# Conditioning products for the second layer's first norm: from the first layer's attention to behind its output projection

## The chip, the cores and the metric

The kernel runs on one core of one Trainium2 chip. The metric is the device time of one execution in microseconds (us); less is better. The core has a matrix engine (TensorE, PE in the views, with its weight loads as PEld), a vector engine (DVE), a scalar engine (ACT), GpSimd (POOL) and a sync engine (SP), which here issues most of the loads from DRAM. Each engine works through its own instructions in order and waits on semaphores for the others.

## The reference

A trunk of two layers over 512 latent tokens and 256 context tokens of width 1024. What matters here is where the conditioning enters:

```python
m = split((silu(c) @ w_ada[l] + b_ada[l]), 6)         # six vectors of 1024 for the latent stream
h = layer_norm(x) * (1 + m[1]) + m[0]                 # first norm, feeds the input projection
y = concat(pool, windowed attention, latent attention, gating)(h @ w_in[l]) @ w_out[l]
x = layer_norm_affine(ALPHA * x + m[2] * y)
f = square(relu((layer_norm(x) * (1 + m[4]) + m[3]) @ w_ff1[l])) @ w_ff2[l]
x = layer_norm_affine(ALPHA * x + m[5] * f)
```

The context stream does the same in the first layer with its own vector `c_ctx`; in the second layer it only needs m[0] and m[1]. `c` is known from the start, so the products with `w_ada` depend on nothing but their weights.

## The kernel before

All products are in float32 or in pairs of float32r halves, so that every weight block is loaded raw by SP (512 KB in one DMA), split on ACT (high half) and DVE (low half), and used three times by TensorE. Raw blocks go through a ring of four slots (tag `raw`); SP issues the next load when a slot is free again.

**Conditioning.** `ada_steps(l, g, ...)` computes 2048 of the 6144 columns of layer l: g = 0 holds the first norm's shift and scale, g = 1 the attention gate and the second norm's shift, g = 2 the second norm's scale and the feed-forward gate. It goes in 16 steps; each loads one raw block of `w_ada` (512 KB, tile `wada`) into the same ring of four and does 8 products on TensorE straight from it (16 matmul instructions in the trace), with no split. The sum lies in one PSUM bank (tile `ada`, a pool with one buffer), and DVE adds the bias (tile `badab`) when a part of it is done, into `adaA` (L250); that frees the bank. `ada_cols` turns the rows into columns with TensorE transposes (`adaT`) and DVE copies; `gate_rows` writes a gate to DRAM (`grow`, issued by SP).

**Where it is done.** The generator `conditioning()` in `run` hands out the steps while the units of attention are written: `fill(x, n)` takes steps up to a number that grows with the unit x. In the first layer these are the 16 steps of g = 1, the first 8 of g = 2, and the 16 of the second layer's g = 0, 40 in all (24 in the second layer). The other 8 steps of g = 2 are written after the output projection (`out_proj`, tiles `wo`), behind the norms `norm1`.

**What follows.** `norm1` runs on DVE, ACT and POOL, tile by tile (tiles `x`, `xc`, `xn`). Then `ffn` starts with `ff1_first`: `modT` transposes the normalised tiles on TensorE (tile `hT`), ACT scales them (`hh`, `hfull`), DVE takes the low half (`hl`), and the first 512 columns of the feed-forward product follow (tile `ff`, weights `w1z` already split). Seven more chunks of 512 follow, with weights through the ring (`raww`).

**What sets the order.** A scheduler of the framework orders the instructions of each engine when the kernel is built, from the order in which the code writes them and a simulated timeline; the order on an engine is then fixed.

Of the kernel before, what the change touches and what calls it, by code (L numbers as in the profile page):

```python
# [14 lines left out]
PSUM = bass.MemoryType.PSUM  # L15
DRAM = bass.MemoryType.DRAM
# [11 lines left out]
# layer norm of ALPHA x + y as that of x + y / ALPHA, with the guard scaled alike  # L28
# [19 lines left out]
class Trunk:  # L48
# [64 lines left out]
    def load(self, **kw):  # L113
        """a load by the sync engine; while self.chain is set, behind the one before."""
        i = self.nc.sync.dma_start(**kw)
        if self.chain is not None:
            if self.chain:
                self.after(i, self.chain[-1])
            self.chain.append(i)
        return i  # L120

# [10 lines left out]
    def split(self, hi, lo, src, scale=None):  # L132
        """hi + lo = src * scale, each half exact in fp32r."""
        nc = self.nc
        if scale is None:
            i = nc.scalar.activation(out=hi, in_=src, func=AF.Copy)
            nc.vector.tensor_tensor(out=lo, in0=src, in1=hi.bitcast(F32), op=ALU.subtract)
            return i
        else:
            nc.scalar.activation(out=hi, in_=src, func=AF.Copy, scale=scale)  # L140
            nc.vector.scalar_tensor_tensor(
                out=lo, in0=src, scalar=scale, in1=hi.bitcast(F32), op0=ALU.mult, op1=ALU.subtract
            )

    def load_w(self, pieces, shape, name, gate=None):
        """weights from DRAM, split in two fp32r halves; pieces: (slice of the tile, source)."""
        nc = self.nc
        raw = self.pr.tile(shape, F32, name=self.nm("raw" + name), tag="raw")
        for sl, src in pieces:
            self.load(out=raw[sl], in_=src)  # L150
        hi = self.pw.tile(shape, F32R, name=self.nm("hi" + name), tag="W")
        lo = self.pw.tile(shape, F32R, name=self.nm("lo" + name), tag="W")
        i = nc.scalar.activation(out=hi, in_=raw, func=AF.Copy)  # L153
        if gate is not None:
            self.after(i, gate)
        nc.vector.tensor_tensor(out=lo, in0=raw, in1=hi.bitcast(F32), op=ALU.subtract)  # L156
        return hi, lo

    def rstd(self, out, var, scale=1.0, eps=EPS):
        """(var * scale + eps) ** -0.5"""  # L160
        nc = self.nc
        v = self.S1("rv")
        nc.vector.tensor_scalar(out=v, in0=var, scalar1=scale, scalar2=eps, op0=ALU.mult, op1=ALU.add)
        nc.gpsimd.tensor_tensor(out=out, in0=v, in1=self.mhalf, op=ALU.pow)

    def stats(self, src, chunks, eps=EPS):
        """mean and 1/std of rows; src(i) gives the i-th chunk of at most 512 columns."""
        nc = self.nc
        st = self.S1("bst", 6 * chunks)
        for i in range(chunks):  # L170
            nc.vector.bn_stats(out=st[:, 6 * i:6 * i + 6], in_=src(i))  # L171
        mv = self.S1("bmv", 2)
        nc.vector.bn_aggr(out=mv, in_=st)
        rs = self.S1("brs")
        self.rstd(rs, mv[:, 1:2], eps=eps)
        return mv[:, 0:1], rs
# [39 lines left out]
    def ada_steps(self, l, g, res, parts=((0, 1, 2, 3),)):  # L216
        """2048 columns of silu(c) @ w_ada + b_ada for both streams, in steps: row 32 j + 16 stream,
        column 128 q + x holds feature 512 q + 128 j + x. The rows go to res[0]."""
# [38 lines left out]
    def ada_cols(self, a, name, plus_one, parts=((0, 1, 2, 3),), mc=None):  # L257
        """columns [feature, block, stream] out of the rows of ada; plus_one: halves that are scales."""
        nc = self.nc
        if mc is None:  # L260
            mc = self.pc.tile([128, 16, 2], F32, name=self.nm(name), tag=name, bufs=2)
        for part in parts:
            pt = self.PA("adaT")
            for i, q in enumerate(part):
                self.tr(pt[:, 128 * i:128 * i + 128], a[:, q, :])
                nc.vector.tensor_scalar(
                    out=mc[:, 4 * q:4 * q + 4, :],
                    in0=pt[:, 128 * i:128 * i + 128].rearrange("p (b r) -> p b r", r=32)[:, :, 0:32:16],
                    scalar1=1.0 if q // 2 in plus_one else 0.0, scalar2=None, op0=ALU.add,
                )  # L270
        return mc

    def gate_rows(self, a, half, streams):
        """1024-wide rows of ada to DRAM, over ALPHA."""
# [30 lines left out]
    def sum_sq(self, x, nm, junk, name):  # L305
        """sum of (x + nm) ** 2 of rows on the scalar engine."""
# [20 lines left out]
    def affine_ln2(self, x, g, b, dst, act):  # L327
        """x = affine layer norm of x, and the plain layer norm of that in dst; act: the latter on the scalar
        engine."""
# [22 lines left out]
    def modT(self, xn, t0, t1, shift, scale, h, kts=range(KT), two=False):  # L352
        """xn(i, kt): token tile i, features kt; fills h[kt] = hi, lo [feature, token]."""
        nc = self.nc
        n = 128 * (t1 - t0)
        for kt in kts:
            pt = (self.PF if two and kt % 2 else self.PA)("hT")
            last = None
            for i in reversed(range(t0, t1)):
                # the last token tile first, so that the bank is not held while it is awaited  # L360
# [56 lines left out]
    def rope(self, x, p0, p1, tab, shuf):  # L417
        """x [p0:p1, 512] in place."""
# [7 lines left out]
    def proj_T(self, l, hL, hC, c0, nf, evict, ctx_too, name):  # L426
        """feature-major columns c0.. of h @ w_in, nf tiles of 128."""
# [26 lines left out]
    def wb_units(self, l, k0, k1, ku, cols, name):  # L454
        """token-major weights of h @ w_in, split: [kt][hi, lo]."""
# [13 lines left out]
    def proj_tok(self, l, groups, cols, ku, evict, name, Ws=(), early=None):  # L469
        """token-major columns of h @ w_in; groups: lists of (h tiles, index in h, output number), each  # L470
        preceded by what prepares it; cols: column ranges."""
        n = sum(b - a for a, b in cols)
        Ws = list(Ws)
        if early is not None:
            # by halves of the features, as the conditioning comes in
# [37 lines left out]
    def softmax(self, S, lo, hi, keep, z=False):  # L513
        """rows of S[:, lo:hi] in PSUM; the first `keep` probabilities come back."""
# [21 lines left out]
    def probs_T(self, p, nb):  # L536
        """transposes the nb key blocks of p."""
# [15 lines left out]
    def pv(self, O, pTs, vs, q0):  # L553
        """O[64 * head : , q0 : q0 + 128] += sum over key blocks of v^T p^T for two heads."""
# [9 lines left out]
    def mixers(self, l, P, hL, hC, preps, fill, early):  # L564
# [6 lines left out]
        # cq and the gating half of the spatial-gating unit, token-major  # L571
# [26 lines left out]
        # pooling  # L598
        pool_finish = self.pool(l, P, hL, hC, yL, yC, full)
        # k and q of the windowed attention  # L600
# [47 lines left out]
        # u  # L648
# [9 lines left out]
        # v, ckv, kr token-major  # L658
# [15 lines left out]
        # spatial gating  # L674
        self.sgu(l, P, U, VG, yL, yC, full)

        # latent attention: normalised low-rank parts, feature-major
# [118 lines left out]
        # the work, one head and one tile of queries at a time  # L796
# [39 lines left out]
        # latent-attention operands are made ahead, between the units of the part before  # L836
# [134 lines left out]
    def ff1_z(self, l):  # L971
        """the weights of the first chunk, split in slots that are free between the phases; three slots
        take the eight blocks of a column tile."""
# [17 lines left out]
    def wb_z(self, l):  # L991
        """the first feature tiles of the weights of the first projection, likewise."""
# [20 lines left out]
    def xn_new(self, ends):  # L1013
        """room for a normalised token tile: a slot, and a third of another."""
# [12 lines left out]
    def out_weights(self, l):  # L1027
        """the first half of w_out, while attention ends."""
# [15 lines left out]
    def out_part(self, yL):  # L1044
        """next products of the first two token tiles that do not wait for the last heads."""
# [7 lines left out]
    def out_proj(self, l, yL, yC, x, xc, gl, gc, gate_inst):  # L1053
        """x += gate (y @ w_out), token-major."""
# [29 lines left out]
    def ffn(self, l, hL, hC, x, xc, rows2, mod2, done):  # L1084
# [40 lines left out]
        def ff1_first():  # L1125
            """the first chunk while the hidden state is still being made: token halves apart, in their
            own banks, so that the first does not wait for the second."""
# [78 lines left out]
    def bcast_rows(self, src, name):  # L1206
        """a parameter row on all partitions, loaded behind the scalar engine's work so far."""
# [5 lines left out]
    def run(self):  # L1213
# [53 lines left out]
        for l in range(DEPTH):  # L1267
# [4 lines left out]
            # conditioning that only the rest of the layer needs, between the units of attention  # L1272
# [3 lines left out]
            def conditioning():  # L1276
# [9 lines left out]
                if not last:  # L1286
                    yield from self.ada_steps(l + 1, 0, r)
                    cond["mc0"] = self.ada_cols(r[0], "mc0", (1,))
# [4 lines left out]
            def fill(x, n):  # L1293
                want = (x + 1) * (24 if last else 40) // (n - 4) + 1
# [7 lines left out]
            gr1, mc0 = cond["gr1"], cond.get("mc0")  # L1302
            # residual stream again
# [29 lines left out]
            # the second gate, while the first norm is awaited  # L1333
            for _ in cond["ada2"]:
                pass
            gr2 = self.gate_rows(cond["a2"], 1, ns)
            norm2 = []
# [12 lines left out]
            def done(j):  # L1350
                """token tile j has left the feed-forward part."""
# [87 lines left out]
```

## Time and profile before

| | |
|---|---|
| runs, us | 1599.86, 1599.83, 1595.42; median 1599.83 |
| profiled execution | span 1596.2 us from the first to the last instruction; no time of its own is listed for it |
| TensorE | busy 1519.9 us (95%) |
| DVE, ACT, POOL | busy 933.6, 573.8, 207.9 us |
| DMA | 169.94 MB, 106 GB/s on average |
| granted TensorE clock | 0.986 of 2.4 GHz on average |

The span falls into stages: projections of the first layer to about 160 us, its attention from 160 to 330, its output projection from 329.4 to 383.95, its feed-forward part from 386 to about 915, and then the same for the second layer, without context queries. Times in the rows are microseconds from the span's start.

### The profile page before, as it was taken

The page shows a single profiled execution, that of the slowest core. Times are in us where ns is not written, and L with a number is a line of the kernel's source. Part 1 is how long each engine was busy: PE and PEld are TensorE (multiplying, and loading weights), DVE is VectorE, ACT ScalarE, POOL GpSimd, SP SyncE. Part 2 cuts the span into 40 slices and gives each one's busy share as a digit, 9 for nine tenths or more (in the row PEclk, how much of TensorE's full clock was granted, in tenths as well). Part 3 has the DMA queues.
Part 4 walks back from the last instruction along what each step waited for, and adds up shares of the span by engine and source line. Part 5 has one row for each costly group of instructions (what it writes and reads, how often), then busy time and mean ns, then how long its engine had stood idle before and what let it go on. Part 6 is the DMA issues. An engine that isn't in the chain of part 4 may idle for free.

```text
span 1596.2 us, 23567 instructions
## 1 busy us (share of the span) xinstructions
PE 1519.9 (95%) x9480; PEld 1257.1 (79%) x9480; DVE 933.6 (58%) x1630; ACT 573.8 (36%) x1003; POOL 207.9 (13%) x217
## 2 busy tenths in 40 slices
PE   5999989999999999999999989998988999999996
PEld 3789767777888888888888868876767888888885
DVE  3484776457445445454454788577546555655557
ACT  4533445423631211312212166346534523223230
POOL 1011223224000000000000151124113000000003
PEclk9999999999999999999999999999999999999999
DMA  9432635363232121221212224260554332332321
GB/s 307 144 117 79 195 115 167 112 237 95 73 97 62 53 79 53 80 62 55 70 53 80 69 90 119 74 205 10 164 188 122 119 105 94 93 93 92 106 80 53
DMA packets 148069, 169.94 MB, mean 106 GB/s; under 512 B 8776, under 2 KB 96248, under 8 KB 147960
## 3 DMA queue, kind: packets, MB, share of 16 engines
q1 hardware_dynamic: 138488, 150.98, 30.4%
q10 hardware_dynamic: 9472, 17.45, 3.2%
q8 instruction: 75, 1.23, 0.3%
q14 instruction: 34, 0.28, 0.1%
HBM read 164.19 MB, written 4.22 MB: 106 GB/s over the span
## 4 chain that ended last, share of the span: by engine, by line
PE 79%; DVE 9%; DMA 6%; ACT 2%; POOL 2%; issue 1%; SPq 0%; ACTq 0%; DVEq 0%; POOLq 0%
PE ff L124 53%; PE wo L124 4%; DMA wada<-in_w_ada 4%; PE wb L124 3%; PE o L124 3%; PE wa L124 2%; PE pT L179 2%; PE ada L124 2%; PE sm L124 2%; PE wu L124 2%; DMA rawwo<-in_w_out 1%; PE hT L179 1%; PE s L124 1%; DVE bst L171 1%; PE wp L124 1%
## 5 line engine op out<-in xcount | busy, mean ns | idle before, releaser
L153 ACT ACTIVATE hiw<-raww 128x1024 fp32r<-128x1024 f32 x120 | 127.1, 1065 | 565.1 <-PE ff L124 565.1
L156 DVE TENSOR_TENSOR low<-raww,hiw 128x1024 fp32r<-128x1024 f32 x120 | 146.4, 1223 | 246.1 <-ACT hiw L153 246.1
L124 PE MATMUL ff<-low,fh 128*128 128x512 f32 x640 | 249.0, 389 | 0.0
L124 PE MATMUL ff<-hiw,fl 128*128 128x512 f32 x640 | 249.0, 389 | 0.0
L124 PE MATMUL ff<-hiw,fh 128*128 128x512 f32 x640 | 247.9, 389 | 0.0
L124 PE MATMUL ff<-hl,hiw 128*128 128x512 f32 (+1 forms) x672 | 237.9, 354 | 0.0
L124 PE MATMUL ff<-hh,hiw 128*128 128x512 f32 (+1 forms) x672 | 237.8, 354 | 0.0
L124 PE MATMUL ff<-hh,low 128*128 128x512 f32 (+1 forms) x672 | 237.7, 354 | 0.0
L1177 DVE TENSOR_TENSOR fft<-ff,gate 128x512 f32<-128x512 f32 x160 | 109.9, 687 | 100.3 <-PE ff L124 100.3
L124 PEld LDWEIGHTS ff<-hh,hiw 128*128 128x128 f32 x672 | 127.1, 189 | 17.9
L124 PEld LDWEIGHTS ff<-hl,hiw 128*128 128x128 f32 x672 | 127.1, 189 | 17.6
L124 PEld LDWEIGHTS ff<-hh,low 128*128 128x128 f32 x672 | 127.0, 189 | 17.6
L124 PEld LDWEIGHTS ff<-hiw,fl 128*128 128x128 f32 x640 | 120.2, 188 | 24.9
L124 PEld LDWEIGHTS ff<-low,fh 128*128 128x128 f32 x640 | 120.2, 188 | 24.7
L124 PEld LDWEIGHTS ff<-hiw,fh 128*128 128x128 f32 x640 | 120.2, 188 | 24.7
L1178 POOL TENSOR_TENSOR x<-x,fft 128x512 f32<-128x512 f32 x16 | 23.2, 1459 | 850.7 <-DVE fft L1177 845.7
L124 PE MATMUL ada<-wada,sc 128*32 128x128 f32 x1536 | 70.4, 301 | 27.4 <-DMA wada<-in_w_ada 14.8
L531 POOL TENSOR_SCALAR p<-p,rec 128x768 f32<-128x768 f32 (+3 forms) x80 | 68.0, 852 | 180.8 <-DVE rec L530 158.8
L124 PEld LDWEIGHTS ada<-wada,sc 128*32 128x32 f32 x1536 | 43.4, 117 | 47.3 <-DMA wada<-in_w_ada 21.9
L1178 DVE TENSOR_TENSOR x<-x,fft 128x512 f32<-128x512 f32 x112 | 77.3, 690 | 2.9
L179 PE MATMUL pT<-ident,p 128*128 128x128 f32 x368 | 62.3, 282 | 7.9 <-DVE rec L530 2.9
L124 PE MATMUL wo<-hiwo,yh 128*128 128x512 f32 x160 | 63.3, 402 | 3.5 <-ACT hiwo L153 3.4
(325 smaller groups left out, 2794.1 us busy)
## 6 DMA issues: line engine op xcount, KB each, us to landing
raww<-in_w_ff SPq DMA_DIRECT2D x120, 512.0 KB, 4.1
wada<-in_w_ada SPq DMA_DIRECT2D x96, 512.0 KB, 5.6
rawwo<-in_w_out SPq DMA_DIRECT2D x16, 512.0 KB, 7.0
rawz<-in_w_ff SPq DMA_DIRECT2D x8, 512.0 KB, 5.1
rawwb<-in_w_in SPq DMA_DIRECT2D x12, 256.0 KB, 3.6
gate<-grow ACTq DMA_DIRECT2D x6, 512.0 KB, 4.0
badab<-in_b_ada SPq DMA_DIRECT2D x36, 64.0 KB, 4.2
x<-in_x SPq DMA_DIRECT2D x4, 512.0 KB, 3.8
```

What stands on the lines that cost most here:

```text
L124: return self.nc.tensor.matmul(out, lhsT, rhs, start=start, stop=stop)
L153: i = nc.scalar.activation(out=hi, in_=raw, func=AF.Copy)
L156: nc.vector.tensor_tensor(out=lo, in0=raw, in1=hi.bitcast(F32), op=ALU.subtract)
L171: nc.vector.bn_stats(out=st[:, 6 * i:6 * i + 6], in_=src(i))
L179: return self.nc.tensor.transpose(out, in_, self.ident if ident is None else ident)
L531: nc.gpsimd.tensor_scalar(out=p[:, :keep], in0=p[:, :keep], scalar1=rec, scalar2=1.0, op0=ALU.mult, op1=ALU.mult)
L1177: nc.vector.tensor_tensor(out=t, in0=ps, in1=g[:, sl], op=ALU.mult)
L1178: eng.tensor_tensor(out=xt[:, sl], in0=xt[:, sl], in1=t, op=ALU.add)
```

## The change

The 16 steps of the second layer's g = 0 leave `conditioning()`. They are written in one go behind the rest of g = 2 and its gate rows, after `norm1` and before `ffn`; their columns `mc0` are made there too. `fill` now spreads 24 steps over attention in both layers. The rest of the difference is comments and docstrings.

```diff
                 mc[2] = self.ada_cols(r[0], "mc2", (0,), ((0, 1),))
                 cond["ada2"], cond["a2"] = ada2, r[0]
-                if not last:
-                    yield from self.ada_steps(l + 1, 0, r)
-                    cond["mc0"] = self.ada_cols(r[0], "mc0", (1,))
...
             def fill(x, n):
-                want = (x + 1) * (24 if last else 40) // (n - 4) + 1
+                want = (x + 1) * 24 // (n - 4) + 1
...
-            gr1, mc0 = cond["gr1"], cond.get("mc0")
+            gr1 = cond["gr1"]
...
             for _ in cond["ada2"]:
                 pass
             gr2 = self.gate_rows(cond["a2"], 1, ns)
+
+            if not last:
+                r1 = [None]
+                for _ in self.ada_steps(l + 1, 0, r1):
+                    pass
+                mc0 = self.ada_cols(r1[0], "mc0", (1,))
             norm2 = []
```

**TensorE, from the last product of the first layer's output projection on.** A row with x8 is one step; the numbers count tiles and differ between the two kernels. Before:

```order
L124 MATMUL wo_4149<-hiwo_4005,yl_3788 128x512
L124 MATMUL ada_4365<-wada_4366,sc 32x128 x8
L124 MATMUL ada_4365<-wada_4376,sc 32x128 x8
L124 MATMUL ada_4365<-wada_4386,sc 32x128 x8
L124 MATMUL ada_4365<-wada_4396,sc 32x128 x8
L179 MATMUL hT_4489<-ident,xn_4237 128x128
...
L124 MATMUL ff_1070_4545<-hh_4177,w1z_3813 128x256
L124 MATMUL ff_1073_4598<-hh_4177,w1z_3835 128x256
L124 MATMUL ada_4365<-wada_4406,sc 32x128 x8
```

And of the change, where the first of 8 rows of `ada_4187` and the first and last of 16 rows of `ada_4280` are shown:

```order
L124 MATMUL wo_3971<-hiwo_3827,yl_3610 128x512
L124 MATMUL ada_4187<-wada_4188,sc 32x128 x8
...
L124 MATMUL ada_4187<-wada_4263,sc 32x128 x8
L124 MATMUL ada_4280<-wada_4281,sc 32x128 x8
...
L124 MATMUL ada_4280<-wada_4436,sc 32x128 x8
L179 MATMUL adaT_4448<-ident,adaA_4279 128x128
L179 MATMUL hT_4489<-ident,xn_4059 128x128
```

Before, four steps stand ahead of the first transpose of the feed-forward part, and the other four among the first feed-forward products. Now all 24 steps, and one `adaT`, stand ahead of the first transpose.

**SP, the loads behind the output projection's last weights (`rawwo`).** Before:

```order
L115 DMA wada_4396<-in_w_ada 128x2x512
L115 DMA badab_4436<-in_b_ada 32x4x128 x2
L115 DMA wada_4406<-in_w_ada 128x2x512
L115 DMA wada_4416<-in_w_ada 128x2x512
L115 DMA wada_4426<-in_w_ada 128x2x512
L115 DMA badab_4436<-in_b_ada 32x4x128 x2
L115 DMA wada_4441<-in_w_ada 128x2x512
L115 DMA raww_1126_4997<-in_w_ff 128x8x128
```

Of the change, from the eighth block on:

```order
L115 DMA wada_4263<-in_w_ada 128x2x512
L115 DMA badab_4431<-in_b_ada 32x4x128 x2
L115 DMA wada_4281<-in_w_ada 128x2x512
...
L115 DMA wada_4311<-in_w_ada 128x2x512
L280 DMA grow_4275<-adaA_2904 4x2x128
L280 DMA grow_4277<-adaA_2904 4x2x128
L115 DMA wada_4321<-in_w_ada 128x2x512
...
L115 DMA wada_4436<-in_w_ada 128x2x512
L115 DMA raww_1126_4997<-in_w_ff 128x8x128
```

Sixteen more blocks and a bias now stand ahead of the first feed-forward weights (`raww`), and the gate rows (`grow`) stand between the twelfth and the thirteenth block.

**DVE, around the additions that free the bank of `ada` (L250).** Before:

```order
L334 SCALAR_TENSOR_TENSOR xc_3799,sm_4326<-xc_3799,brs_4321,ln1b_3809 128x1024
L372 TENSOR_TENSOR hl_4182<-hfull_4506,hh_4181 128x256
L372 TENSOR_TENSOR hl_4184<-hfull_4513,hh_4183 128x256
L337 TENSOR_SCALAR sm_4326<-sm_4326 128x1
L250 TENSOR_TENSOR adaA_2494<-ada_4365,badab_4436 128x256
```

Of the change:

```order
L334 SCALAR_TENSOR_TENSOR xc_3621,sm_4148<-xc_3621,brs_4143,ln1b_3631 128x1024
L337 TENSOR_SCALAR sm_4148<-sm_4148 128x1
L250 TENSOR_TENSOR adaA_2904<-ada_4187,badab_4258 128x256
L277 TENSOR_SCALAR adaA_2904<-adaA_2904 128x256
L250 TENSOR_TENSOR adaA_4279<-ada_4280,badab_4431 128x512
L266 TENSOR_SCALAR mc_1020_4447<-adaT_4448 128x8 x2
L372 TENSOR_TENSOR hl_4000<-hfull_4492,hh_3999 128x256
```

The addition that frees the bank for the moved steps stands behind the first context tile's affine norm (L334, `xc`); the addition over the moved steps stands ahead of every `hl`.

In attention the 16 steps of g = 1 keep their places on TensorE. The 8 of g = 2 move later, to where the moved steps began; the stretch where they stood has no step left.

## Rows read from the trace of the kernel before

**Rows 1.** The page: engine totals, the conditioning's products, its loads (KB, median us to landing).
```profile
PE 1519.9 (95%) x9480; PEld 1257.1 (79%) x9480; DVE 933.6 (58%) x1630; ACT 573.8 (36%) x1003; POOL 207.9 (13%) x217
...
L124 PE MATMUL ada<-wada,sc 128*32 128x128 f32 x1536 | 70.4, 301 | 27.4 <-DMA wada<-in_w_ada 14.8
...
wada<-in_w_ada SPq DMA_DIRECT2D x96, 512.0 KB, 5.6
```

**Rows 2.** Busy us by stretch, feed-forward: PE, PEld, DVE, ACT, POOL, granted clock, DMA share, GB/s.
```profile
480.00:520.00 40.00, 40.00 (x190) 33.59 (x189) 22.73 (x30) 6.85 (x7) 0.00 (x0) 1.00 0.19 59
```

**Rows 3.** The same view, four stretches of the first layer's attention.
```profile
185.50:221.84 36.34, 31.10 (x242) 23.83 (x242) 27.00 (x72) 21.06 (x50) 12.94 (x16) 1.00 0.13 40
221.84:256.00 34.16, 32.16 (x336) 24.10 (x339) 21.36 (x49) 15.19 (x35) 10.58 (x11) 1.00 0.41 133
256.00:278.00 22.00, 21.49 (x323) 15.01 (x313) 11.67 (x29) 11.21 (x26) 5.63 (x7) 1.00 0.84 281
278.00:288.20 10.20, 8.30 (x95) 6.09 (x87) 6.61 (x11) 6.51 (x10) 1.91 (x2) 1.00 0.74 234
```

**Rows 4.** Waits of TensorE, 222 to 256 us, then 256 to 305 (us, times, longest).
```profile
PE ada L124 <- DVE adaA L250: 1.5, 1, 1.5
PE ada L124 <- DMA wada<-in_w_ada: 1.1, 2, 0.6
...
PE ada L124 <- DMA wada<-in_w_ada: 1.6, 3, 1.2
```

**Rows 5.** TensorE in order of time behind the output projection: start, us, instructions [idle before].
```profile
383.95 1.95 PE L124 MATMUL ada<-wada,sc 128*32 128x128 f32 x64
385.84 0.66 PE L179 MATMUL hT<-ident,xn 128*128 128x128 f32 x4
...
388.45 0.65 PE L124 MATMUL ada<-wada,sc 128*32 128x128 f32 x16 [0.35 <-DMA wada<-in_w_ada]
...
391.79 0.58 PE L124 MATMUL ff<-hl,w1z 128*128 128x256 f32 x1 [2.33 <-DVE hl L372]
...
392.94 1.08 PE L124 MATMUL ada<-wada,sc 128*32 128x128 f32 x16
```

**Rows 6.** Busy us by stretch, from the first transpose on (columns as in Rows 2).
```profile
385.84:404.40 18.56, 14.18 (x136) 11.15 (x132) 15.16 (x39) 12.02 (x27) 5.17 (x7) 0.82 0.79 233
404.40:440.00 35.60, 33.95 (x262) 31.56 (x263) 13.26 (x26) 23.58 (x49) 0.55 (x1) 1.00 0.19 60
```

**Rows 7.** SP's queue: issues of conditioning blocks, start, us over which they went.
```profile
350.88 5.47 SPq L115 DMA_DIRECT2D wada<-in_w_ada  x4
...
384.66 1.41 SPq L115 DMA_DIRECT2D wada<-in_w_ada  x3
```

**Rows 8.** TensorE at the kernel's start, eight conditioning steps and nothing else.
```profile
10.79 1.08 PE L124 MATMUL ada<-wada,sc 128*32 128x128 f32 x16 [10.79 <-DVE sc L202]
12.02 1.08 PE L124 MATMUL ada<-wada,sc 128*32 128x128 f32 x16 [0.15 <-DMA wada<-in_w_ada]
...
14.73 1.08 PE L124 MATMUL ada<-wada,sc 128*32 128x128 f32 x16 [0.27 <-DMA wada<-in_w_ada]
16.07 1.08 PE L124 MATMUL ada<-wada,sc 128*32 128x128 f32 x16 [0.27 <-DMA wada<-in_w_ada]
18.73 1.08 PE L124 MATMUL ada<-wada,sc 128*32 128x128 f32 x16 [1.58 <-DMA wada<-in_w_ada]
...
23.05 1.08 PE L124 MATMUL ada<-wada,sc 128*32 128x128 f32 x16 [1.37 <-DMA wada<-in_w_ada]
24.77 0.45 PE L179 MATMUL adaT<-ident,adaA 128*128 128x128 f32 x1 [0.64 <-DVE adaA L250]
```

**Rows 9.** GB/s of all DMA in 40 slices of the first 30 us.
```profile
GB/s 0 0 7 70 175 371 404 393 421 421 412 388 407 393 393 391 380 390 374 382 358 374 328 373 279 196 251 333 325 369 332 348 336 380 396 385 393 399 391 385
```

**Rows 10.** DVE in order of time behind the output projection.
```profile
395.01 1.28 DVE L334 SCALAR_TENSOR_TENSOR xc<-xc,brs,ln1b 128x1024 f32<-128x1024 f32 x1
...
398.72 0.42 DVE L250 TENSOR_TENSOR adaA<-ada,badab 128x256 f32<-128x256 f32 x1 [1.69 <-PE ada L124]
```

## The prediction

> **What bounds the kernel.** I read the page first: TensorE is busy for 1519.9 of 1596.2 us [rows 1], so a microsecond of its queue is a microsecond of the kernel wherever it has no slack. The busy time by stretch says where that is. In the feed-forward part it has none: 40.00 of 40 us [rows 2], at a DMA share of 0.19 and with DVE and ACT far from full. Whatever delays the start of that part therefore arrives at the end undiminished. In the first layer's attention there is some slack: of the 102.70 us in the four stretches, 93.05 are busy, and the idle part is uneven [rows 3]. From 185.5 to 221.84, where almost no conditioning stands, 5.24 of 36.34 us are idle (14%); from 221.84 to 278, where most of the steps stand, 2.51 of 56.16 (4%). So the steps there are partly filler: they run while attention waits for its softmax chain.
>
> Next I read what TensorE does behind the output projection [rows 5]. The last product is followed at 383.95 by four conditioning steps in 1.95 us, whose blocks were loaded long before (issued from 350.88 on, [rows 7]), and at 385.84 by the first transpose of the feed-forward part. The next three blocks are issued only at 384.66, when these four free their slots, and the first of them is used at 388.45. The ring of four is thus the only prefetch there is: four blocks can be in SBUF when the projection ends, and every further one costs a trip to DRAM.
>
> **What the change does, step by step.** I call T the end of the output projection (383.95 before) and split the sum in three.
>
> *A, what attention gives back.* Sixteen steps leave it. A step takes 0.49 us back to back (64 instructions in 1.95 us) to 0.65 alone [rows 5], so 7.8 to 10.4 us, with 9.1 in the middle; four `adaT` leave too, at no more than the 0.45 us of [rows 8] each, for which I take 1.2 together. Waits for conditioning blocks were 1.1 and 1.6 us, and one for the bank 1.5 [rows 4]; eight steps with their loads remain, so I credit 1.5 of these 4.2. Against that, the stretch from 221.84 to 256 loses its filler. If it becomes as idle as the one before it, 14% of the remaining some 27 us is 3.8 us, against 2.0 idle now, of which the bank's wait and the loads' were most; I charge 2.5. A = 9.1 + 1.2 + 1.5 - 2.5 = 9. Bounds: 7.8 and 1.2 with no credit and 4 charged gives 5; 10.4 + 1.2 + all of 2.7 gives 14.
>
> *S, what the feed-forward part waits.* In the change, 24 steps stand ahead of the first transpose on TensorE, which works in order. The first four go as before, T to T + 1.95. The fifth block needs its slot, a load and its landing; before, that took until 388.45, T + 4.5. From there the ring decides. Its cycle, from a step to the one that uses the same slot again, is read at the kernel's start, where TensorE also does nothing but these steps [rows 8]: 10.79 to 16.07 is 5.28 us, 12.02 to 18.73 is 6.71, and 14.73 to 23.05 is 8.32 (with a bias and other loads in between). The median landing of 5.6 us [rows 1] and 1.08 us for the step, as it runs there, also make 6.7. I take 6.7.
> - Step 8 begins at T + 1.5 + 6.7 = T + 8.2 and ends by about T + 9.
> - Step 9 needs the PSUM bank, which DVE frees with its addition. That stands in DVE's order behind the affine norm of the first context tile, which began at 395.01 and took 1.28 [rows 10]: T + 12.4, and 0.42 for the addition: T + 12.8. The norms do not depend on the moved work, so this time stays. The ring is full by then, so steps 9 to 12 go at 1.08 us each and the twelfth begins at T + 16.2.
> - Three more turns of the ring: the 24th begins at T + 16.2 + 3 x 6.7 = T + 36.3.
> - From the start of the last step to `adaT` it is 1.72 us at the start of the kernel (23.05 to 24.77); the first transpose follows at T + 38.2.
>
> Before, it came at T + 1.9, so S = 36. SP's gate rows hold nothing up: they wait for the same addition, and the slot for the thirteenth block is free only after it. Bounds: without the wait for the bank and with the shortest cycle, T + 1.5 + 5 x 5.28 + 1.9 = T + 29.8, S = 28; with the longest, T + 16.2 + 25 + 1.9, S = 41. The DMA engines as such would allow less: 421 GB/s [rows 9] are 1.25 us a block, 25 us for twenty; with 4.5 for the first landing that again is about 28.
>
> The Trainium skill, page "DMA: Bandwidth & Descriptors", section "Where 436 GB/s comes from", says that about 358 GB/s of HBM per core binds for loads from HBM (a table beside it has more for one core alone); by that figure twenty blocks would take 29.3 us, an estimate from that page. This trace disagrees, with 421; by the page S could not be under some 32, and the sum not under +9.
>
> *G, what the stage behind it gets back.* Before, the stretch from the first transpose to 404.4 held four steps (two of 0.65 and two of 1.08, 3.5 us) and 18.56 - 14.18 = 4.4 us idle [rows 6], 2.33 of it in one wait for `hl` behind the norms on DVE [rows 5]. After a delay of 36 us the latent tiles' norms are long done, so I take all but 1 us of that idle as gone, and charge 0.9 for the `adaT` there now. G = 3.5 + 3.4 - 0.9 = 6. Its granted clock averaged 0.82: the steps at 1.08 us in place of 0.65 are its time at 1.2 GHz, behind the idle time at 389 to 391.8. 18.56 x 0.36 makes 6.7 us at the low level and 3.3 us lost. I assume the same loss behind the stream of blocks. Bounds: 2 if the low clock lasts twice as long, 9 if it isn't lost at all.
>
> No cover is left for these steps but the norms, which end about 12 us after T. The weights of the next feed-forward chunk queue behind the moved blocks on SP and in the ring; TensorE needs them only behind the first chunk, which takes over 50 us from the first transpose (the two stretches of [rows 6]), so they keep far ahead.
>
> **The sum.** S - A - G = 36 - 9 - 6 = +21 us. On the profiled span that is 1596.2 + 21 = 1617; the median of the runs is 3.6 us above that span, so the same on the median is 1599.8 + 21 = 1621. Within 0.3% (4.8 us) I call the time the same; that is about what a measurement of this kernel can tell.
>
> **The rivals.**
> - *The ring feeds faster and attention gives back more.* With all bounds on the good side: 28 - 14 - 9 = +5, 1605. For it speaks that DMA reached 421 GB/s at the start; against it, that the ring at that same place took up to 8 us a turn. For all that comes out under +9 in this way: 7%, of which 1% is no change.
> - *The clock stays low behind the stream.* TensorE has a step of 0.5 to 1.1 us every 1.7 us for some 30 us, and comes back with transposes and short products. If the clock is at 1.2 GHz for 22 us behind the first transpose in place of the 6.7 of before, the loss grows from 3.3 to 11 us: +8, 1629. For it: the steps at the start also ran at 1.08 us with DMA waits between them. Against: from 404.4 on the granted clock is 1.00 again [rows 6], although transposes and short products filled the time before. 12%. The Trainium skill, "TensorE: Matmul & The Clock Gate", section "HAM oscillation — how this bites in real kernels", has the rule that a stretch whose products are shorter than the wait for the next block starts each block cold; no other number here hangs on it.
> - *The other side: attention was held up by the loads alone.* All of the four stretches' idle time (9.65 us) goes, with 11.6 us of steps and `adaT`: A = 21. With G at 9 this needs S under 30 to be no slower, and under 25 to be faster by 0.3%; at S = 28 it gives -2, 1598. Against it: the idle time is largest where no steps stand. 3% no change, 2% faster.
> - *The order doesn't hold the moved steps back*, since TensorE would run the transposes first: excluded by TensorE's fixed order.
>
> **Chances and range.** The forecast at +9 to +29 holds 76%, the low clock 12% above it or at its top, the fast ring 7%, the last 5%. Slower 0.94, the same 0.04, faster 0.02. The range reaches from 1609 (+9) to 1633 (+33), which leaves out most of the fast ring and the outer bounds.
>
> **What would show it.** In the profile of the changed kernel, the last `wo` product should end near 375; a lone run of 20 steps behind waits for `wada` should follow, in groups, with one wait for `adaA` between the eighth and the ninth; the first `hT` should start near 413 and the stretch behind it be shorter by some 6 us. From there every stage should lie about 21 us later than before. I am wrong if the blocks come at 1.3 us or less each, if attention ends before 370 or after 379, or if the feed-forward part has slack that takes the delay up.

## The result, and the profile after

| | before | after |
|---|---|---|
| median of four runs each, us | 1597.99 | 1623.49 |
| ratio | | 1.0157, 95% interval 1.0139 to 1.0175 |
| profiled execution, us | span 1596.2 | 1620.67, span 1618.7 |
| TensorE busy, us | 1519.9 | 1524.9 |

The change makes the kernel 25.5 us slower (22 to 28 by the interval); 1621 us was forecast. The page of the kernel after, engine totals and the conditioning's products and loads, answers to [rows 1]:

```profile
PE 1524.9 (94%) x9480; PEld 1259.9 (78%) x9480; DVE 933.8 (58%) x1630; ACT 573.3 (35%) x1003; POOL 208.1 (13%) x217
...
L124 PE MATMUL ada<-wada,sc 128*32 128x128 f32 x1536 | 75.6, 325 | 40.8 <-DMA wada<-in_w_ada 40.8
...
wada<-in_w_ada SPq DMA_DIRECT2D x96, 512.0 KB, 5.1
```

The same 1536 products take 5.2 us more (301 to 325 ns each), and the idle time ahead of them is up from 27.4 to 40.8 us. That is only part of the loss, because steps that were filler in attention now stand alone. TensorE in order of time behind the output projection shows where (compare [rows 5]):

```profile
375.34 0.39 PE L124 MATMUL wo<-hiwo,yl 128*128 128x512 f32 x1
375.65 1.95 PE L124 MATMUL ada<-wada,sc 128*32 128x128 f32 x64
380.03 0.64 PE L124 MATMUL ada<-wada,sc 128*32 128x128 f32 x16 [2.42 <-DMA wada<-in_w_ada]
381.36 0.64 PE L124 MATMUL ada<-wada,sc 128*32 128x128 f32 x16 [0.69 <-DMA wada<-in_w_ada]
383.95 1.08 PE L124 MATMUL ada<-wada,sc 128*32 128x128 f32 x16 [1.95 <-DMA wada<-in_w_ada]
386.68 1.08 PE L124 MATMUL ada<-wada,sc 128*32 128x128 f32 x16 [1.65 <-DMA wada<-in_w_ada]
389.09 1.08 PE L124 MATMUL ada<-wada,sc 128*32 128x128 f32 x16 [1.33 <-DMA wada<-in_w_ada]
390.91 1.08 PE L124 MATMUL ada<-wada,sc 128*32 128x128 f32 x16 [0.74 <-DMA wada<-in_w_ada]
392.26 1.08 PE L124 MATMUL ada<-wada,sc 128*32 128x128 f32 x16 [0.27 <-DMA wada<-in_w_ada]
393.87 1.08 PE L124 MATMUL ada<-wada,sc 128*32 128x128 f32 x16 [0.53 <-DMA wada<-in_w_ada]
...
413.21 1.08 PE L124 MATMUL ada<-wada,sc 128*32 128x128 f32 x16 [0.78 <-DMA wada<-in_w_ada]
415.11 0.47 PE L179 MATMUL adaT<-ident,adaA 128*128 128x128 f32 x1 [0.81 <-DVE adaA L250]
415.38 1.06 PE L179 MATMUL hT<-ident,xn 128*128 128x128 f32 x4
```

Every step behind the first four waits for its block. From the ninth (389.09) to the 24th (413.21) it is 24.12 us for 15 blocks, 1.61 us each. The first transpose of the feed-forward part starts 39.7 us after the first conditioning step behind the projection, where it was 1.9.

The ledger by marks of the two traces:

| mark on TensorE | before | after |
|---|---|---|
| first step behind the projection (T) | 383.95 | 375.65 |
| first `hT` | 385.84 | 415.38 |
| first product of the second feed-forward chunk (`hiw`) | 440.86 | 464.21 |
| last feed-forward product, first layer | 935.30 | 958.65 |
| span | 1596.2 | 1618.7 |

So attention gives 8.3 us back, the wait for the first `hT` costs 39.7 - 1.9 = 37.8, the stage from `hT` to `hiw` is 6.2 shorter (55.02 to 48.83). The sum is +23.3. Then almost nothing takes it up: +23.35 at the end of the feed-forward part and +22.5 in the span. (That part lasts to 935.30 in the trace of before, not to about 915 as I had it ahead of the prediction.)

The busy time by stretch in attention, as [rows 3], then the stream and the stages behind it, as [rows 6] (PE, PEld, DVE, ACT, POOL, granted clock, DMA share, GB/s):

```profile
221.84:256.00 34.16, 32.38 (x233) 25.20 (x233) 24.84 (x54) 20.32 (x48) 13.49 (x15) 0.95 0.03 9
256.00:278.00 22.00, 17.81 (x233) 13.17 (x232) 10.31 (x22) 8.75 (x18) 1.86 (x3) 1.00 0.71 227
...
390.91:413.21 22.30, 15.14 (x224) 8.35 (x225) 0.00 (x0) 0.00 (x0) 0.00 (x0) 0.50 0.94 317
415.38:432.50 17.12, 16.21 (x110) 14.81 (x110) 7.75 (x24) 12.25 (x27) 1.85 (x3) 0.86 0.29 73
432.50:464.21 31.71, 30.07 (x232) 27.69 (x231) 12.69 (x22) 21.42 (x43) 0.00 (x0) 1.00 0.21 68
```

In the stream nothing works but TensorE and DMA. DVE, ACT and POOL have no instruction from 390.91 to 413.21; DVE's next is the addition over the moved steps, at 414.36. TensorE is at its lower level there, 0.50 of 2.4 GHz.

### The profile page after: what moved, and what is told of

The parts are those of the page before. It is cut to its first block, busy times and chain, and to the rows that moved or that the text cites. A ratio compares the mean times of both kernels' runs of the same rounds, so it can differ in the third digit from the quotient of the medians.

```text
span 1618.7 us, 23564 instructions
## 1 busy us (share of the span) xinstructions
PE 1524.9 (94%) x9480; PEld 1259.9 (78%) x9480; DVE 933.8 (58%) x1630; ACT 573.3 (35%) x1003; POOL 208.1 (13%) x217
## 4 chain that ended last, share of the span: by engine, by line
PE 83%; DVE 6%; DMA 6%; ACT 2%; issue 2%; POOL 1%; SPq 0%; ACTq 0%; DVEq 0%; POOLq 0%
PE ff L124 52%; PE wo L124 6%; DMA wada<-in_w_ada 4%; PE wb L124 4%; PE o L124 3%; PE wa L124 2%; PE pT L179 2%; PE ada L124 2%; PE wu L124 2%; PE wp L124 2%; PE sm L124 2%; PE wq L124 2%; PE hT L179 1%; PE wk L124 1%; PE s L124 1%
## 5 line engine op out<-in xcount | busy, mean ns | idle before, releaser
L124 PE MATMUL ada<-wada,sc 128*32 128x128 f32 x1536 | 75.6, 325 | 40.8 <-DMA wada<-in_w_ada 40.8
```

The lines of the kernel that those rows point to most:

```text
L124: return self.nc.tensor.matmul(out, lhsT, rhs, start=start, stop=stop)
```

## The experiments

All ratios are to the kernel before, timed on the same chip. "Wait" is the time from the last `wo` product to the first `hT` (2.2 us before, 40.0 after). Differences in microseconds below are worked out from the ratios; the plain medians of the same runs lie up to 4.3 us from them.

| run | ratio (95% interval) | wait, us |
|---|---|---|
| the change | 1.0157 (1.0139 to 1.0175) | 40.0 |
| e1_left_out | 0.9940 (0.9924 to 0.9957) | 2.2 |
| e2_half | 1.0021 (1.0007 to 1.0035) | 2.4 |
| e3_one_block | 1.0044 (1.0025 to 1.0064) | 23.9 |
| e4_own_bank | 1.0146 (1.0127 to 1.0165) | 39.7 |
| e5_wide | 1.0153 (1.0128 to 1.0177) | 41.2 |
| e5_wide2 | 1.0188 (1.0169 to 1.0207) | 46.5 |
| f1_cols_later | 1.0033 (1.0018 to 1.0048) | 2.2 |
| f3_cols_bank | 1.0032 (1.0015 to 1.0049) | 2.2 |
| f2_behind_chunk | 1.0153 (1.0129 to 1.0176) | 2.2 |
| e6_in_ffn | 1.0038 (1.0022 to 1.0054) | 2.2 |
| e6_cols_later | 0.9995 (0.9983 to 1.0008) | 2.2 |
| e7_spread | 1.0004 (0.9992 to 1.0017) | 2.2 |

**The moved steps left out.**

```diff
-                for _ in self.ada_steps(l + 1, 0, r1):
-                    pass
-                mc0 = self.ada_cols(r1[0], "mc0", (1,))
+                mc0 = mc[1]
```

> The moved 16 steps are left out altogether (the second layer's first norm takes other conditioning columns in their place), so this is the change without S. Theory (the loss is the wait of the feed-forward part behind the steps, attention gives back some 9 us): 8 to 10 us faster than the kernel before, about 1589 us, ratio near 0.994, with the last wo product near 375 and the first hT about 2 us behind it as before. Rival (attention gives less back over several runs than the one trace showed): 3 to 5 us faster. If it is not faster than before at all, the delay has another source than the stream of steps.

0.6% faster, 9.6 us (7 to 12 by the interval; the plain medians, 1591.02 and 1596.35, lie only 5.3 apart). What attention gives back is real and of the size of A; the whole loss comes from where the steps went.

**Half of them moved.** Eight of the 16 steps go through `fill` again, eight stay behind the projection, in two parts of 1024 columns.

```diff
+                    cond["ada0"] = self.ada_steps(l + 1, 0, cond["r1"], ((0, 1), (2, 3)))
+                    for _ in range(8):
+                        yield next(cond["ada0"])
```

> Eight of the 16 moved steps go back into attention, eight stay behind the projection. Theory (each block behind the projection costs one ring period, 1.61 us in the trace of the change): the first hT comes 8 x 1.6 = 13 us earlier than in the change and attention gives back about half, 4.5 us; 25.5 - 13 + 4.5 = 17 us slower than before, ratio near 1.011. Rival (attention gives back most of its 9 us with the first steps removed, or none): 13 or 21 us slower.

A miss on both sides: 3.4 us slower, not 13 to 21. In its trace only four steps stand ahead of the first `hT`, as before, and the others among the transposes and products, with 0.6 us of waits for blocks in all. One `adaT` stands ahead of the first `hT` too, as in the change:

```profile
383.56 0.33 PE L179 MATMUL adaT<-ident,adaA 128*128 128x128 f32 x1
383.73 0.38 PE L179 MATMUL hT<-ident,xn 128*128 128x128 f32 x2
```

But the sums are now made in two parts, and the first was finished in attention, so this `adaT` has no step to wait for. The edit thus changes more than the number of moved steps. The pace of the blocks was no cost there. So the number of moved blocks alone does not set the loss; it matters where TensorE's order puts the transposes. Half the steps cost an eighth of the loss.

**One block for all moved steps.** Fifteen of the 16 loads are gone.

```diff
+                    if not one or (i == 0 and u == 0):
                         wt = self.pr.tile([128, 2, 512], F32, name=self.nm("wada"), tag="raw")
                         self.load(out=wt, in_=w[:, 2 * u:2 * u + 2, c0:c0 + 512])
```

> The 16 moved steps keep their products on TensorE but all use one block, so that 15 of the 16 loads are gone (the columns are then wrong). Theory (the blocks' loads set the pace of the stream): the bank for the moved steps comes free near T + 13 as in the change, 16 steps at 1.08 us follow, and the first hT comes near T + 31 in place of T + 39.7; some 8 us less than the change, 17 us slower than before. Rival (TensorE's products and the wait for the bank set the pace, the loads are hidden): as the change, 25 us slower, T + 39 to 40.

A miss: 7 us slower, so the loads carry some 18 of the 25.5 us, more than I gave them. TensorE's view shows what I had missed:

```profile
386.89 1.08 PE L124 MATMUL ada<-wada,sc 128*32 128x128 f32 x16 [1.56 <-DMA wada<-in_w_ada]
389.53 8.57 PE L124 MATMUL ada<-wada,sc 128*32 128x128 f32 x256 [1.56 <-DMA wada<-in_w_ada]
398.90 0.33 PE L179 MATMUL adaT<-ident,adaA 128*128 128x128 f32 x1 [0.79 <-DVE adaA L251]
```

Without waits the 16 steps run in 8.57 us, 0.54 each, where I had them at 1.08. The granted clock is 0.72 from 389.53 to 394 and 1.00 from there to 398.1, where it was 0.50 in the change's stream. The idle time between blocks costs twice: itself, and the lower level of the clock in the products between.

**The accumulation in a bank of its own.**

```diff
-            ps = self.PF("ada")
+            ps = (bank or self.PF)("ada")
```

> The 16 moved steps accumulate in a bank of the pool of three, so that the ninth step needn't wait for DVE's addition over the first eight. TensorE's order is that of the change. Theory (the ninth step waits for its block anyway, which lands 1.0 us after the addition ends): 0 to 1 us less than the change, ratio near 1.015. Rival (the prediction's step: the bank holds the ninth step, and with it one turn of the ring): 4 us less, ratio near 1.013.

The wait is 39.7 us against 40.0, and the interval overlaps that of the change. The ninth step begins 13.5 us after the last `wo` product here and 13.75 in the change. So the bank did not hold it; in the change its wait ends with the landing of its block. (The row of this run names DVE, `[1.74 <-DVE adaA L277]`; that instruction and the landing end within 0.2 us of each other here.) SP's queue of the change shows when the block was issued:

```profile
380.73 0.38 SPq L115 DMA_DIRECT2D wada<-in_w_ada  x1
381.33 2.90 SPq L115 DMA_DIRECT2D badab<-in_b_ada  x2
384.36 3.83 SPq L115 DMA_DIRECT2D wada<-in_w_ada  x3
388.82 1.09 SPq L280 DMA_DIRECT2D grow<-adaA  x2
390.34 18.50 SPq L115 DMA_DIRECT2D wada<-in_w_ada  x12
```

The gate rows (`grow`) stand between the twelfth and the thirteenth block, so the three blocks ahead of them are the tenth to the twelfth, and the ninth is the one issued at 380.73. Its step begins 8.4 us later (7.8 in this run, issued at 378.77), where the median block lands in 5.1; four blocks and four bias loads were issued ahead of it from 376.36 on. That these made it late was not tried by itself. The last two bias loads keep SP for 2.9 us, 2.0 of them in a wait for an earlier block to land, and so hold up the tenth block, whose slot was free at 382.0. The addition that frees the bank began at 388.05 and took 0.42, so the bank was free 0.6 us before the ninth step began.

**More blocks under way.** The moved blocks go to the eight slots of the split weights; in a second run their loads also keep the order of the code on SP.

```diff
-                        wt = self.pr.tile([128, 2, 512], F32, name=self.nm("wada"), tag="raw")
+                        wt = pool.tile([128, 2, 512], F32, name=self.nm("wada"), tag="W")
```

> The blocks of the 16 moved steps go to the eight slots of the split weights, which the projection has just left, in place of the ring of four; up to twelve blocks can then be under way. Theory (four blocks in flight set the pace: 1.61 us a block): the pace falls toward 1.25 us a block (the 421 GB/s of the kernel's start) or to TensorE's 1.08, the first hT near T + 30, some 9 us less than the change, 16 us slower than before. Rival (DMA itself does no better here than one block in 1.6 us): no gain, 25 us slower than before.

> As the run with eight more slots, but the loads keep the order of the code on SP, so that the first eight blocks come first and the moved sixteen behind them. TensorE's order is that of the change. Theory now (the DMA engines themselves are full in the stream, at a share of 0.94 to 1.0 and 317 to 339 GB/s, so that more blocks under way land no sooner): pace 1.4 to 1.6 us a block behind the ninth, first hT near T + 36 to 40, 21 to 26 us slower than before. Rival (the ring of four sets the pace, as the prediction has it): 1.08 to 1.25 us a block, first hT near T + 30, 16 us slower than before.

Neither is faster than the change, the second is slower than I expected by either theory. In the first, SP's order put eleven conditioning loads into the projection, where the slots came free late: the fifth step waited 8.8 us for its block. In the second, the ring of four was free for the feed-forward weights, so four blocks of them (`raww`, issued from 388.18) came ahead of the last eight conditioning blocks (402.08), and one step waited 7.93 us. What the second shows is the pace where more blocks are under way. By stretch (columns as above):

```profile
390.00:396.00 6.00, 4.46 (x80) 3.19 (x72) 0.01 (x1) 0.00 (x0) 0.00 (x0) 0.50 1.05 385
396.00:402.00 6.00, 3.24 (x48) 1.78 (x48) 0.00 (x0) 0.00 (x0) 0.00 (x0) 0.50 1.18 305
402.00:408.00 6.00, 0.00 (x0) 0.00 (x0) 0.00 (x0) 0.00 (x0) 0.00 (x0) 0.50 1.02 320
408.00:414.00 6.00, 4.33 (x64) 2.38 (x64) 0.00 (x0) 0.00 (x0) 0.00 (x0) 0.50 1.05 379
```

From 396 to 408, where the feed-forward weights come in between, DMA moves 305 to 320 GB/s, about what it moved in the change's stream (317), at a higher share. In that stream it is the ring that sets the pace: ahead of each of its last twelve loads SP waits for TensorE to free a slot, and a block lands 4.7 us after its issue (the change from 390 to 410, SP's waits, then the time to landing):

```profile
SPq L115 <- PE ada L124: 12.5, 12, 1.1
...
DMA to landing us min/median/max: 4.6/4.7/5.5
```

But the DMA engines are near full already. At 385 GB/s, the best stretch here, a block takes 1.36 us, 0.25 less than the change's 1.61; for twenty blocks that is 5 us, an estimate of what a wider ring could take back of the 25.5. How the whole stream would do with the slots and with the weights kept behind it was not tried.

**Only the columns moved.** The steps stay where the change writes them. Only the call of `ada_cols`, four transposes, is written behind the first feed-forward chunk:

```diff
-                mc0 = self.ada_cols(r1[0], "mc0", (1,))
...
         cur = ff1_first()
+        first()        # mc0 = self.ada_cols(r1[0], "mc0", (1,))
```

> The 16 moved steps stay where the change writes them; only the four transposes that turn their rows into columns (adaT, in the pool of three PSUM banks from which the transposes hT of the feed-forward part also take theirs) are written behind the first feed-forward chunk. With that, 4 steps stand ahead of the first hT on TensorE, not 24, and the others among the transposes and products. Theory now (the loss is the order: with adaT written ahead of hT, the hT come behind the whole stream of blocks, and the stream's time is only for that reason exposed): S falls to 0, attention gives back 9.5 us, 16 steps at 0.55 to 0.65 us cost 8.8 to 10.4, waits for blocks 1 to 4 more: 1 to 5 us slower than before, ratio near 1.002. Rival (the rate of the loads holds the feed-forward part up wherever its transposes stand, as TensorE works in order): more than 12 us slower, ratio above 1.008.

**Only the bank of the columns changed.** Nothing is moved in the code at all:

```diff
-            pt = self.PA("adaT")
+            pt = (bank or self.PA)("adaT")
...
-                mc0 = self.ada_cols(r1[0], "mc0", (1,))
+                mc0 = self.ada_cols(r1[0], "mc0", (1,), bank=self.PF)
```

> Nothing moves in the code against the change; the four adaT of the moved steps take their PSUM bank from the pool with one buffer (where the steps accumulate) in place of the pool of three from which hT takes its banks. Then hT doesn't come behind adaT in the order of that pool, and TensorE's order has 4 steps ahead of the first hT, not 24. Theory (banks of one pool are handed out in the order in which the code asks, and that is what put the transposes behind the stream): first hT near T + 2, 3 to 7 us slower than before, ratio near 1.003. Rival (where the columns are written matters for another reason than the bank): as the change, 25 us slower.

Both take four fifths of the loss away: 1.0033 and 1.0032. TensorE in order of time in the run with the columns moved:

```profile
375.76 1.95 PE L124 MATMUL ada<-wada,sc 128*32 128x128 f32 x64
377.65 0.66 PE L179 MATMUL hT<-ident,xn 128*128 128x128 f32 x4
379.24 0.44 PE L179 MATMUL hT<-ident,xn 128*128 128x128 f32 x2 [0.94 <-DVE wot L1081]
380.40 0.64 PE L124 MATMUL ada<-wada,sc 128*32 128x128 f32 x16 [0.48 <-DMA wada<-in_w_ada]
...
400.06 0.64 PE L124 MATMUL ada<-wada,sc 128*32 128x128 f32 x16
...
413.81 1.08 PE L124 MATMUL ada<-wada,sc 128*32 128x128 f32 x16 [3.07 <-DMA wada<-in_w_ada]
```

The first `hT` is back right behind four steps, and the same blocks arrive while transposes and feed-forward products run; waits for blocks fall from 15.9 to 4.3 us. What put the transposes behind the stream is therefore that `adaT` asks for a bank of the pool of three ahead of `hT`, while its columns wait for all the moved steps. The run with half the steps fits: there `adaT` came first as well, but early. The scheduler's order is in keeping with handing out the banks of one pool in the order in which the code asks; that rule was read from the orders, not from the scheduler itself.

**All moved work behind the first chunk's code.** The call of the steps goes where the columns went.

> All of the moved work, steps and columns, is written behind the first feed-forward chunk. Steps behind the projection stand as before (4 ahead of the first hT), the moved ones among the context tiles' transposes and the first chunk's second half. Theory (order): as the run with the columns alone moved, 0 to 5 us slower than before. Rival (the loads' rate): more than 10 us slower.

A miss: the first `hT` comes at once, but the loss is the same as the change's. TensorE, later in the same chunk:

```profile
424.05 1.29 PE L124 MATMUL ada<-wada,sc 128*32 128x128 f32 x38
...
444.17 1.96 PE L124 MATMUL ada<-wada,sc 128*32 128x128 f32 x64
451.46 1.08 PE L124 MATMUL ada<-wada,sc 128*32 128x128 f32 x16 [5.33 <-DMA wada<-in_w_ada]
454.75 1.08 PE L124 MATMUL ada<-wada,sc 128*32 128x128 f32 x16 [2.21 <-DMA wada<-in_w_ada]
```

The moved steps begin only at 424.05. Written there, they ask for the one bank of their pool behind the chunk's fourth product, which uses it too (that this is what holds them was not tried by itself). Then the ring of four has the first blocks ready and the rest must come while TensorE waits: 12.3 us of waits, and from 440 to 480 a granted clock of 0.70. It is a loss of the change's kind in another place: a run of steps longer than the ring.

**Among the feed-forward chunks.** Three steps to a chunk, through a callback in the loop over chunks; then the same with the columns one chunk later.

```diff
             nxt = ff1(c + 1) if c + 1 < NCH else None
+            between(c)     # 3 steps; mc0 = ada_cols(...) at c == 5, in the second run at c == 6
             ff2(c, cur)
```

> The moved steps are written three to a feed-forward chunk, in chunks 0 to 5. TensorE has no idle time there, so 16 steps at 0.53 us, the time of one in the run with one block, cost 8.5 us; attention gives back 8.3 to 9.5: the same as before within 2 us, ratio near 0.9995. Rival (a block of conditioning among the weights in the ring of four makes weights late): 5 us or more slower, with TensorE waits for hiw or loww in the chunks.

> As the run with three steps to a feed-forward chunk, but the columns are made one chunk later, so that TensorE doesn't wait 3.6 us there for DVE's addition. Theory (a step costs TensorE its own 0.5 us wherever nothing waits, in attention and in the feed-forward part alike): 16 x 0.51 = 8.2 us more in the chunks, some 9 less in attention, the same as before within 2 us, ratio 0.999 to 1.001. Rival (attention's gain is partly lost again in what surrounds it): 2 to 4 us slower.

The first is 6 us slower. No weights were late; the one wait of TensorE from 440 to 940 shows in two of its rows:

```profile
804.57 0.64 PE L124 MATMUL ada<-wada,sc 128*32 128x128 f32 x16
808.84 0.33 PE L179 MATMUL adaT<-ident,adaA 128*128 128x128 f32 x1 [3.62 <-DVE adaA L250]
```

TensorE stands 3.62 us before `adaT`, until DVE comes to the addition. Behind it the granted clock is 0.85 from 808.8 to 820, where it is 1.00 before and after, an estimated 1.7 us more. One chunk later that wait is gone, and the time is that of before, 0.9995 (0.9983 to 1.0008). Three steps take 1.52 us there, so 16 cost 8.1 us, which is what attention gives back there (8.5 to 9.0 in the two traces, from its first score product to the last `wo`).

**The kernel before with its steps held to their units.** Each step is ordered behind the scores of the unit at which it is written.

```diff
+                            if self.hold is not None:
+                                self.after(f, self.hold)
```

> The kernel before, with each of its 40 steps in attention held behind the scores of the unit between which it is written, so that the steps lie where attention has idle time (5.24 of 36.34 us in the stretch from 185.5) in place of standing in clusters. Theory (steps fill the waits of softmax): 2 to 4 us faster than before, ratio near 0.998. Rival (the waits are short and each step makes a product of attention late): the same or 1 to 3 us slower.

No difference, 1.0004. TensorE is busier in 155 to 222 (61.2 us against 59.1) but attention ends no sooner. No version here that does all the work beats the kernel before.

## Why the prediction was right, step by step

- **A**, forecast 9: 8.3 at T, 9.5 counted from the first score product of attention (154.36 before, 155.52 after, to the last `wo` at 383.63 and 375.34), 9.6 by the run without the steps. By terms, from the first score product to the first step behind the projection, before and after (columns as above):

```profile
154.36:383.95 229.59, 216.72 (x1927) 167.44 (x1925) 143.00 (x321) 100.56 (x221) 69.87 (x71) 0.99 0.45 148
155.52:375.65 220.13, 205.35 (x1667) 160.76 (x1665) 142.11 (x316) 100.07 (x221) 68.42 (x71) 0.99 0.35 115
```

TensorE is busy for 11.4 us less, where I had 10.3 for the steps and `adaT`, and idle for 1.9 more, where I had 1.0 (2.5 charged, 1.5 credited). The two errors cancel. The charge for lost filler did not fall where I put it, as far as the same times can be compared with other work in them: 221.84 to 256 stays busy (32.38 us), while 256 to 278 falls from 21.49 to 17.81.
- **S**, forecast 36: 37.8. The ring was right: every load of the stream waits for a slot, and four blocks take 6.4 us where I had 6.7. What I had not seen is that the DMA engines are close behind it, with a wider ring worth some 0.25 us a block. The way into the ring was wrong. The bank came free at T + 12.8, as forecast, but the ninth step came at T + 13.4 because it waited for its block, and with a bank of its own it came no earlier; that the two times lie so close is luck. I also had the ring full by then and the twelfth step at T + 16.2; the next three waited for their blocks too, and it came at T + 18.2. The three turns behind it took 19.3 us where I had 20.1, so part of the error cancels.
- **G**, forecast 6: 6.2. The granted clock was 0.86 in the first 17 us, where it was 0.82 in the 18.56 of before, so the loss of clock did not grow.
- **The sum**, forecast +21: +23.3 by the marks, +22.5 in span, +25.5 between the medians (1597.99 before, with a fourth run; I had 1599.83 from three).
- **The rivals.** The fast ring and the loads-only attention are out: S was 37.8, and A 9, not 14 or 21. The low clock behind the stream is out by the 0.86 above. The Trainium skill's rule for it ("TensorE: Matmul & The Clock Gate", section "HAM oscillation — how this bites in real kernels") speaks of products shorter than the waits; in the stream the steps are longer than most waits (1.08 us against 0.25 to 1.62 behind the ninth) and the granted clock was 0.50 all the same, so there the trace goes further than the rule.
- **What the prediction did not ask** is why the transposes stand behind all 24 steps. It read the order and took it as part of the move. The runs show that the move itself costs 5 us (1.0033, 1.0032), and that the other 20 hang on one PSUM bank, taken by four transposes ahead of the feed-forward part's.

## What to carry to other kernels

Moving work that needs blocks from DRAM is cheap as long as it stands among other work, and dear as soon as more of it than the ring holds stands in a row on an engine that works in order. Look in the order for what comes ahead of the next stage, and then for why: here it was a PSUM bank that a small later step asked for too early, and another bank cured most of it. Where the receiving stage is full, as the feed-forward part is here, a moved step cost there what it gave back, and the best case was no change.

## What the hardware showed that was not expected

- A DMA share near 1 did not mean one rate: 317 GB/s at 0.94 in the change's stream, 385 at 1.05 with more blocks under way, and 305 at 1.18 with feed-forward weights among them.
- The same conditioning step takes 1.08 us with waits of 0.25 to 1.62 us before it and 0.54 us in an unbroken run of 16, in the same stage.
- One execution's attention is no fine measure. The runs with the columns moved and with their bank changed have the same TensorE order there; the granted clock from 256 to 305 was 1.00 in one profile and 0.86 in the other, and the last `wo` product came at 375.45 and 380.67. Their medians are 0.2 us apart. In the ten profiles with the change's TensorE order there, the time from the first score product to the last `wo` product runs from 218.3 to 225.4 us, with 220.3 in the middle, against 229.3 in the one trace of before: A is 9 by the middle, 4 to 11 by single traces.
